# Layer 1's GLU, u and short-conv projections: three 256-column matmuls a block become one of 512 columns and one of 256

## Chip, cores and metric

The kernel runs on one core of one Trainium2 chip. The metric is the device time of one execution in microseconds; the time before is the median of three runs. On the core five engines work side by side: TensorE (PE, whose weight loads are listed apart as PEld), VectorE (DVE), ScalarE (ACT), GpSimd (POOL) and SyncE (SP), which issues the DMAs. TensorE multiplies a stationary block of at most 128 x 128 with moving columns and writes into PSUM, of which one bank holds 512 fp32 columns of 128 partitions. VectorE and ScalarE read PSUM and write SBUF.

## What is computed

A two-layer encoder trunk on 256 positions with 2048 features, in fp32. The part that matters here is the first half of each layer: one input projection `h @ w_in`, whose 4288 columns are split among four mixers.

```python
IN_WIDTHS = (2 * W_G, Q_LORA, KV_LORA, MLA_ROPE, W_G, W_G, W_G, 2 * W_G)   # W_G = 512
h = layer_norm(x) * (1.0 + scale_m) + shift_m
proj = h @ w_in[l]
uv, q_c, kv_c, k_r, sb, sc, sh, ag = jnp.split(proj, IN_SPLITS, axis=-1)
y_a = gmlp_mixer(uv, ...)               # gelu(u) * (W_s LN(gelu(v)) + b)
y_b = mla_mixer(q_c, kv_c, k_r, ...)    # latent attention, 4 heads
y_c = short_conv_mixer(sb, sc, sh, w)   # sb * conv3(sc * sh)
y_d = conformer_conv(ag, ...)           # silu(LN(conv31(a * sigmoid(g))))
y = jnp.concatenate([y_a, y_b, y_c, y_d], axis=-1) @ w_out[l]
x = layer_norm(ALPHA * x + (1.0 + gate_m) * y, post_mix_g[l], post_mix_b[l])
```

Then a gated FFN follows (`ffn_w_up`, a width-3 conv on the gate, SiLU, `ffn_w_down`), with a post-norm of the same kind. The modulation vectors (shift, scale, gate) come from `silu(c) @ w_mod[l]`.

## The kernel before

**Products in three terms.** fp32 products run on TensorE in a faster 32-bit format (`F32R`). For this each weight tile and each activation tile is split into a high part (a cast to F32R on ScalarE, line 460 for weights, 479 for activations) and a low part (the rest, a subtraction on VectorE, lines 461 and 480). A product is high x high + high x low + low x high. Weights arrive as a 1 MB raw tile of 128 partitions x 2048 columns (`weights`, DMA on line 446, four buffers shared with the modulation's weights), and are split into two tiles of 1024 columns; there are four buffers for the high and four for the low ones.

**Activations.** `act_pair` holds two K tiles of the transposed, normalised input `hT` in one tile, ordered (K tile, high or low, 256 positions). So the high and low part of one K tile lie side by side in 512 columns.

**Groups.** Layer 1's `mixers` runs the input projection as groups over 16 K tiles (2048 features), each followed by a function that takes its PSUM tiles:

- V (`first_group`): 512 columns of the gMLP's v, in plain fp32, laid into the norm that ends layer 0
- D: the 1024 columns `ag` (`mix_d`: sigmoid of g, times a, then 31 conv taps for each of four channel blocks, put on the background list)
- U: 512 columns of u (`mix_u`: GELU; `mix_v`: the spatial gating)
- B: 704 columns of the latents (`latent_group`; `mix_b`: the whole attention)
- C: the 1024 columns `sc` and `sh` (`mix_c`: their product, then the width-3 conv)
- E: 512 columns `sb` (`mix_e`: times C's result)

D, U, C and E use `group` (line 482). Its channel blocks of 128 columns take 256 PSUM columns each, two blocks to a bank, and for each K tile and block it issues the three terms as three matmuls of 256 columns (lines 506 to 508). D and C hold four banks and read units of two K tiles x 1024 columns; U and E hold two and read units of four K tiles x 512. The FFN's up projection uses `group2` (line 533) instead: 512 weight columns in units of four K tiles, one bank for each of the four blocks. Per K tile and block it issues a matmul of the high weights with both halves of the activations (512 columns: high x high on the left, high x low on the right) and one of the low weights with the high activations (256 columns, added on the left). Afterwards ScalarE copies the right half out (`second`, line 1339) and VectorE adds it to the left (lines 1346 and 1376). In a unit, blocks 0 and 1 go through all four K tiles before blocks 2 and 3.

**Order.** `stream` issues a unit's load and splits, then the products of the unit before, then a share of modulation work (`pump`, by `RATES`: in layer 1 one step a unit in D, none in U, B and C, 0.9 in E) and up to `bg` items of the background list (`STEPS`). A group's finishing function is issued after the first load of the next group. The engines' instruction streams are ordered at compile time by a list scheduler that follows this order as priority and moves on to other ready work where an instruction would wait in its model; each engine then runs its own stream strictly in order. A modulation step (line 240) multiplies a 128 x 2048 tile of `w_mod` into a sum on VectorE.

**Buffers.** The pool `accp` has six PSUM banks for groups and output products, `msp` two for small things. The pool `slot` has eleven SBUF tiles of 128 x 1024, `tmp` four of 128 x 512. After E, `out_proj` (line 666) starts with four accumulator banks, two for each half of the positions, and multiplies the four mixers' results in the order a, b, c, d.

Layer 0 goes through `by_pieces` and keeps its own form.

Of the kernel before, what the change touches and what calls it, by code (L numbers as in the profile page):

```python
# [9 lines left out]
AF = mybir.ActivationFunctionType  # L10
ALU = mybir.AluOpType
# [3 lines left out]
D = 2048  # L15
S = 256
# [9 lines left out]
C_UV, C_Q, C_SB, C_SC, C_AG = 0, 1024, 1728, 2240, 3264  # L26
# [24 lines left out]
def encoder_kernel(ctx: ExitStack, tc: tile.TileContext, A: dict, consts: bass.AP, out: bass.AP):  # L51
# [17 lines left out]
    def tmp_tile(name):  # L69
        return tmpp.tile([P, 512], F32, tag="tmp", name=name)  # L70
# [13 lines left out]
    def slot(name, dtype=F32):  # L84
        return slotp.tile([P, 1024], dtype, tag="slot", name=name)
# [396 lines left out]
    def group(w, c0, width, name, then, ntm=0, nk=2, hF=None, bg=0, spare=0):  # L482

        ncm = (width - 512 * ntm) // P
        box = {}

        def products(item, u):
            if u == 0:  # L490
                box["c"] = [acc_tile(f"{name}_c{i}") for i in range((ncm + 1) // 2)]
                box["t"] = [[acc_tile(f"{name}_t{t}{i}") for i in range(ntm)] for t in range(2)]
                box["h"] = list(hT)
            for part in (range(0, min(4, ncm)), range(4, ncm)):
                for k, (hi, lo) in enumerate(item):
                    kt = u * nk + k
                    st, sp = kt == 0, kt == KT - 1
                    for i in part:
                        o = box["c"][i // 2][:, (i % 2) * S : (i % 2 + 1) * S]
                        off = slice(i * P, (i + 1) * P)  # L500
                        first = st and i % 2 == 0
                        if lo is None:
                            mm(o, hi[:, off], hF(kt), first, sp)
                        else:
                            xh, xl = (h[:, kt % 2, :] for h in box["h"][kt // 2][:2])
                            mm(o, hi[:, off], xh, first, False)
                            mm(o, hi[:, off], xl, False, False)
                            mm(o, lo[:, off], xh, False, sp)
            for k, (hi, lo) in enumerate(item):
                kt = u * nk + k  # L510
                st, sp = kt == 0, kt == KT - 1
                for i in range(ntm):
                    off = slice(ncm * P + i * 512, ncm * P + (i + 1) * 512)
                    for t in range(2):
                        tok = slice(t * P, (t + 1) * P)
                        o = box["t"][t][i]
                        if lo is None:
                            mm(o, hF(kt)[:, tok], hi[:, off], st, sp)
                        else:
                            xh, xl = (h[:, kt % 2, tok] for h in box["h"][kt // 2][:2])  # L520
                            mm(o, xh, hi[:, off], st, False)
                            mm(o, xh, lo[:, off], False, False)
                            mm(o, xl, hi[:, off], False, sp)

        def load(u, spare=spare):
            return weights(w, u * nk, nk, c0, width, hF is not None, spare if u == 0 else 0)

        def end():
            then(box["c"], box["t"])

        return KT // nk, load, products, end, bg

    def group2(w, c0, name, then, bg=0, spare=0):


        nk = 4
        box = {}

        def products(item, u):
            if u == 0:  # L540
                box["c"] = [acc_tile(f"{name}_c{i}") for i in range(4)]
                box["h"] = list(hT)
            for part in (range(0, 2), range(2, 4)):
                for k, (hi, lo) in enumerate(item):
                    kt = u * nk + k
                    both = box["h"][kt // 2][2][:, kt % 2, :, :]
                    for i in part:
                        o = box["c"][i]
                        off = slice(i * P, (i + 1) * P)
                        mm(o, hi[:, off], both.rearrange("p h t -> p (h t)"), kt == 0, False)  # L550
                        mm(o[:, :S], lo[:, off], both[:, 0, :], False, kt == KT - 1)

        def load(u):
            return weights(w, u * nk, nk, c0, 512, False, spare if u == 0 else 0)

        return KT // nk, load, products, lambda: then(box["c"]), bg
# [60 lines left out]
    def run(g):  # L617
        units, load, products, end, bg = g
        for u in range(units):
            stream(lambda: load(u), lambda item, u=u: products(item, u), bg)  # L620
        pending.append(end)
# [223 lines left out]
    def mixers(l, w_in, Y, hF=None, between=None):  # L845
# [10 lines left out]
        def mix_d(cps, _):  # L856
            glu = slot("gluD").rearrange("p (j s) -> p j s", j=4)
            for b in range(2):
                sg = tmp_tile("sg")
                act.activation(out=sg, in_=cps[2 + b], func=AF.Sigmoid)  # L860
                dve.tensor_tensor(
                    out=glu[:, 2 * b : 2 * b + 2, :],
                    in0=cps[b].rearrange("p (j s) -> p j s", j=2),
                    in1=sg.rearrange("p (j s) -> p j s", j=2),
                    op=ALU.mult,
                )
            yd = slot("convD").rearrange("p (j s) -> p j s", j=4)
            def tap(j, k):
                if k == 30:
                    ident_act(yd[:, j, :], glu[:, j, :], CW(30, j), CB(j))  # L870
                else:
                    dve.scalar_tensor_tensor(  # L872
                        out=yd[:, j, 30 - k :],
                        in0=glu[:, j, : S - 30 + k],
                        scalar=CW(k, j),
                        in1=yd[:, j, 30 - k :],
                        op0=ALU.mult,
                        op1=ALU.add,
                    )

            for j in range(4):
                for k in range(30, -1, -1):
                    background.append(lambda j=j, k=k: tap(j, k))
            background.append(lambda: norm_d(yd))
# [38 lines left out]
        def mix_u(cps, _):  # L923
            Y["a"] = slot("ya").rearrange("p (j s) -> p j s", j=4)
            for b in range(2):
                act.activation(
                    out=Y["a"][:, 2 * b : 2 * b + 2, :],
                    in_=cps[b].rearrange("p (j s) -> p j s", j=2),
                    func=AF.Gelu_apprx_tanh,
                )  # L930

        def gelu_v(t, ps):
            if t == 0:
# [229 lines left out]
        def mix_c(cps, _):  # L1163
            ch = slot("chC").rearrange("p (j s) -> p j s", j=4)
            for b in range(2):
                sc = tmp_tile("sc")
                act.copy(sc, cps[b])
                dve.tensor_tensor(
                    out=ch[:, 2 * b : 2 * b + 2, :],
                    in0=cps[2 + b].rearrange("p (j s) -> p j s", j=2),  # L1170
                    in1=sc.rearrange("p (j s) -> p j s", j=2),
                    op=ALU.mult,
                )
            yc = Y["c"] = slot("yc").rearrange("p (j s) -> p j s", j=4)
            for j in range(4):
                act.activation(out=yc[:, j, :], in_=ch[:, j, :], func=AF.Copy, scale=SW(2, j))
                for k in range(2):
                    dve.scalar_tensor_tensor(
                        out=yc[:, j, 2 - k :],
                        in0=ch[:, j, : S - 2 + k],  # L1180
                        scalar=SW(k, j),
                        in1=yc[:, j, 2 - k :],
                        op0=ALU.mult,
                        op1=ALU.add,
                    )

        def mix_e(cps, _):
            yc = Y["c"]
            for b in range(2):
# [4 lines left out]
                    op=ALU.mult,  # L1194
                )

        if hF is not None:
            return by_pieces(l, w_in, hF, between, mix_d, mix_u, gelu_v, mix_v, mix_b, mix_c, mix_e)
        phase(l, "V")
        first_group(w_in, C_UV + 512, gelu_v)  # L1200
        phase(l, "D")
        run(group(w_in, C_AG, 1024, f"D{l}", mix_d))

        def mix_uv(cps, _):
            mix_u(cps, None)
            mix_v()

        phase(l, "U")
        run(group(w_in, C_UV, 512, f"U{l}", mix_uv, nk=4, bg=STEPS[l]["U"]))
        phase(l, "B")  # L1210
        run(latent_group(w_in, C_Q, f"B{l}", mix_b, bg=STEPS[l]["B"]))
        phase(l, "C")
        run(group(w_in, C_SC, 1024, f"C{l}", mix_c, bg=STEPS[l]["C"]))
        phase(l, "E")
        run(group(w_in, C_SB, 512, f"E{l}", mix_e, nk=4, bg=STEPS[l]["E"]))
        drain_background()

    def by_pieces(l, w_in, hF, between, mix_d, mix_u, gelu_v, mix_v, mix_b, mix_c, mix_e):
# [360 lines left out]
```

## Time and profile before

| | |
|---|---|
| time, median of 3 runs | 2282.23 us (2279.70, 2282.23, 2286.89) |
| profiled execution, span | 2283.6 us (its device time is not given apart) |
| layer 0's FFN up projection | about 480 to 960 us |
| norm between the layers, V | 1190.0 to 1231.7 us |
| layer 1: D, U | 1231.7 to 1278.0, 1278.0 to 1301.5 us |
| layer 1: B, C with the attention | 1301.5 to 1334.8, 1334.8 to 1413.5 us |
| layer 1: E | 1413.5 to 1441.3 us |
| matmuls of the listed groups D, U, C, E in layer 1 | 384 + 192 + 384 + 192 |
| HBM read | 600.11 MB, 264 GB/s over the span |

How to read it: times in the trace are microseconds from the start of the span, durations of single instructions mostly nanoseconds. A group's line gives its source line, engine, operation, tile written and tiles read, shapes and count, then busy time and mean duration, then the idle time before its instructions and what ended it. All matmuls of the products are issued by one helper on line 79, so they are told apart by the tile they write: `D_c`, `U_c`, `B_w` and `B_n`, `C_c`, `E_c` for the groups, `g_c` and `v_c` for the FFN's gate and value, `o` and `d` for the two output projections. A row of the stage table gives for each engine its busy time and number of instructions, then TensorE's granted clock, the DMA engines' busy share and GB/s. Matmuls are pipelined, and their ends are modelled.

### The profile page before, as it was taken

The numbers are of one execution on the slowest core, as the hardware profiler recorded it, in microseconds if no ns is written. First come the engines' busy times: TensorE is split into PE (matmuls) and PEld (weight loads), VectorE is DVE, ScalarE is ACT, GpSimd is POOL, SyncE is SP. The second block draws the span as 40 slices with busy tenths as digits, with TensorE's granted clock in tenths as the row PEclk, the third lists the DMA queues.
The fourth block names the chain that finished last, engine by engine and source line by source line (L and its number), as shares of the span: only waits on it lengthen the run. The fifth ranks groups of instructions, "written<-read, shape, count | busy, mean of one in ns | idle before, by whom it ended". The sixth has DMA issues, their size and how long they took to land. (4 is left out here: it accounts for less than half of the span.)

```text
span 2283.6 us, 29677 instructions
## 1 busy us (share of the span) xinstructions
PE 2218.9 (97%) x11502; PEld 1846.1 (81%) x11502; DVE 1785.1 (78%) x2258; ACT 1056.0 (46%) x1551; POOL 38.8 (2%) x61
## 2 busy tenths in 40 slices
PE   5799999999999999999999999999999999999998
PEld 4687786478888888887886989877888888888886
DVE  6868899588889898998977896887776565665676
ACT  2231241354554554544556444556555554454553
POOL 1000000000000000000000000000000000000000
PEclk9999999999999999999999999999999999999999
DMA  9999879878898989988875664866765556555554
GB/s 348 357 325 329 321 284 378 316 261 322 307 334 302 330 307 329 322 316 297 322 271 191 236 193 161 322 244 227 247 222 184 191 182 200 186 195 190 193 194 148
DMA packets 224565, 604.15 MB, mean 265 GB/s; under 512 B 14548, under 2 KB 27076, under 8 KB 202660
## 3 DMA queue, kind: packets, MB, share of 16 engines
q1 hardware_dynamic: 223576, 601.25, 74.2%
q8 instruction: 90, 1.47, 0.3%
q0 software_dynamic: 848, 1.01, 0.1%
q14 instruction: 51, 0.42, 0.1%
HBM read 600.11 MB, written 2.10 MB: 264 GB/s over the span
## 5 line engine op out<-in xcount | busy, mean ns | idle before, releaser
L461 DVE TENSOR_TENSOR wlo<-wraw,whi 128x1024 fp32r<-128x1024 f32 (+1 forms) x624 | 748.1, 1212 | 307.6 <-ACT whi L460 301.1
L460 ACT CAST whi<-wraw 128x1024 fp32r<-128x1024 f32 (+1 forms) x624 | 649.3, 1046 | 724.5 <-PE g_c L79 198.8
L79 PE MATMUL v_c<-hT,whi 128*128 128x512 f32 x1408 | 491.3, 393 | 0.0
L79 PE MATMUL g_c<-hT,whi 128*128 128x512 f32 x1280 | 446.8, 393 | 0.0
L79 PE MATMUL v_c<-hT,wlo 128*128 128x256 f32 x1408 | 393.9, 280 | 0.0
L79 PE MATMUL d<-whi,a 128*128 128x512 f32 x1344 | 387.7, 390 | 0.0
L240 DVE SCALAR_TENSOR_TENSOR macc<-wmod,cact,macc 128x2048 f32<-128x2048 f32 x150 | 351.7, 2344 | 19.1 <-DMA wmod<-in_w_mod_dram 18.6
L79 PE MATMUL g_c<-hT,wlo 128*128 128x256 f32 x1280 | 358.2, 280 | 0.0
L79 PEld LDWEIGHTS v_c<-hT,whi 128*128 128x128 f32 x1408 | 263.7, 187 | 59.7
L79 PEld LDWEIGHTS d<-whi,a 128*128 128x128 f32 x1344 | 252.8, 188 | 52.5
L79 PEld LDWEIGHTS g_c<-hT,whi 128*128 128x128 f32 x1280 | 239.7, 187 | 54.4
L79 PEld LDWEIGHTS v_c<-hT,wlo 128*128 128x128 f32 x1408 | 265.8, 189 | 0.2
L79 PEld LDWEIGHTS g_c<-hT,wlo 128*128 128x128 f32 x1280 | 241.7, 189 | 0.2
L79 PE MATMUL d<-wlo,a 128*128 128x512 f32 x672 | 233.8, 390 | 1.9 <-DVE wlo L461 1.9
L79 PEld LDWEIGHTS d<-wlo,a 128*128 128x128 f32 x672 | 126.6, 188 | 29.0 <-DVE wlo L461 2.7
L79 PE MATMUL o<-whi,a 128*128 128x512 f32 x352 | 101.7, 396 | 1.4 <-ACT whi L460 1.4
L872 DVE SCALAR_TENSOR_TENSOR convD<-gluD,pm,convD 128x255 f32<-128x255 f32 (+22 forms) x240 | 98.3, 460 | 0.4
L479 ACT CAST a<-g 128x512 fp32r<-128x512 f32 x132 | 81.1, 616 | 35.4 <-PE d L79 32.7
L79 PE MATMUL D_c<-hT,whi 128*128 128x256 f32 x448 | 88.0, 297 | 3.8 <-ACT hT L479 3.0
L480 DVE TENSOR_TENSOR a<-g,a 128x512 fp32r<-128x512 f32 x132 | 87.6, 683 | 1.8 <-ACT a L479 1.8
L604 PE MATMUL first<-wexact,hN 128*128 128x512 f32 x192 | 85.7, 596 | 1.5 <-ACT hN L82 1.2
L240 DVE SCALAR_TENSOR_TENSOR qacc<-wmod,cact,qacc 128x1024 f32<-128x1024 f32 (+1 forms) x75 | 80.2, 1070 | 2.4 <-DMA wmod<-in_w_mod_dram 0.4
(324 smaller groups left out, 2462.5 us busy)
## 6 DMA issues: line engine op xcount, KB each, us to landing
wraw<-in_ffn_w_up_dram SPq DMA_DIRECT2D x168, 1024.0 KB, 5.1
wmod<-in_w_mod_dram SPq DMA_DIRECT2D x160, 1024.0 KB, 6.6
wraw<-in_ffn_w_down_dram SPq DMA_DIRECT2D x88, 1024.0 KB, 5.2
wmod<-in_w_mod_dram SPq DMA_DIRECT2D x64, 512.0 KB, 8.2
wraw<-in_w_in_dram SPq DMA_DIRECT2D x30, 1024.0 KB, 7.1
wexact<-in_w_in_dram SPq DMA_DIRECT2D x52, 512.0 KB, 7.0
wraw<-in_w_out_dram SPq DMA_DIRECT2D x24, 1024.0 KB, 6.8
wexact<-in_w_out_dram SPq DMA_DIRECT2D x16, 512.0 KB, 11.8
```

What stands on the lines that cost most here:

```text
L79: pe.matmul(o, lhsT, rhs, start=start, stop=stop, skip_group_check=True)
L240: i = dve.scalar_tensor_tensor(out=acc, in0=w, scalar=col, in1=acc, op0=ALU.mult, op1=ALU.add)
L460: held(act.copy(hi[:, :m], r), "cast")
L461: i = dve.tensor_tensor(out=lo[:, :m], in0=r, in1=hi[:, :m].bitcast(F32), op=ALU.subtract)
L479: act.copy(hi, src)
L480: dve.tensor_tensor(out=lo, in0=src, in1=hi.bitcast(F32), op=ALU.subtract)
L604: i = pe.matmul(ps, hN[kt // 4][:, kt % 4, t * P : (t + 1) * P], parts[kt], start=kt == 0, stop=kt == KT - 1, skip_group_check=True,)
L872: dve.scalar_tensor_tensor(out=yd[:, j, 30 - k :], in0=glu[:, j, : S - 30 + k], scalar=CW(k, j), in1=yd[:, j, 30 - k :], op0=ALU.mult, op1 ...
```

## The change

In layer 1 alone, D, U, C and E go through `group2`. D is run as two groups of 512 columns, first g (`Dg`), then a (`Da`); C as sc (`Cc`), then sh (`Ch`). The new `joined` copies the right half of each bank into a `tmp` tile and adds the left half, and yields two blocks at a time; the finishing functions use it. `Dg` ends with the sigmoid into the GLU's slot, `Da` multiplies into it and starts the conv; `Cc` ends with its sum in the slot `chC`, `Ch` multiplies into it and starts the short conv. The tails `conv_d` and `conv_c` are the old code under a name. The rates and the number of units stay.

```diff
+            conv_d(glu)
+
+        def joined(cps):
+
+            for b in range(2):
+                t = tmp_tile("second").rearrange("p (j s) -> p j s", j=2)
+                for i in range(2):
+                    act.copy(t[:, i, :], cps[2 * b + i][:, S:])
+                    dve.tensor_tensor(out=t[:, i, :], in0=cps[2 * b + i][:, :S], in1=t[:, i, :], op=ALU.add)
+                yield b, t
+
+        def gated_d(cps):
+            Y["glu"] = slot("gluD").rearrange("p (j s) -> p j s", j=4)
+            for b, t in joined(cps):
+                act.activation(out=Y["glu"][:, 2 * b : 2 * b + 2, :], in_=t, func=AF.Sigmoid)
+
+        def valued_d(cps):
+            glu = Y.pop("glu")
+            for b, t in joined(cps):
+                g = glu[:, 2 * b : 2 * b + 2, :]
+                dve.tensor_tensor(out=g, in0=g, in1=t, op=ALU.mult)
+            conv_d(glu)
+
+        def conv_d(glu):
...
+        def joined_u(cps):
+            Y["a"] = slot("ya").rearrange("p (j s) -> p j s", j=4)
+            for b, t in joined(cps):
+                act.activation(out=Y["a"][:, 2 * b : 2 * b + 2, :], in_=t, func=AF.Gelu_apprx_tanh)
...
+            conv_c(ch)
+
+        def first_c(cps):
+            Y["ch"] = slot("chC").rearrange("p (j s) -> p j s", j=4)
+            for i in range(4):
+                ch = Y["ch"][:, i, :]
+                act.copy(ch, cps[i][:, S:])
+                dve.tensor_tensor(out=ch, in0=cps[i][:, :S], in1=ch, op=ALU.add)
+
+        def second_c(cps):
+            ch = Y.pop("ch")
+            for b, t in joined(cps):
+                c = ch[:, 2 * b : 2 * b + 2, :]
+                dve.tensor_tensor(out=c, in0=c, in1=t, op=ALU.mult)
+            conv_c(ch)
+
+        def conv_c(ch):
...
+        def joined_e(cps):
+            for b, t in joined(cps):
+                c = Y["c"][:, 2 * b : 2 * b + 2, :]
+                dve.tensor_tensor(out=c, in0=c, in1=t, op=ALU.mult)
...
         phase(l, "D")
-        run(group(w_in, C_AG, 1024, f"D{l}", mix_d))
-
-        def mix_uv(cps, _):
-            mix_u(cps, None)
+        run(group2(w_in, C_AG + 512, f"Dg{l}", gated_d))
+        run(group2(w_in, C_AG, f"Da{l}", valued_d))
+
+        def mix_uv(cps):
+            joined_u(cps)
             mix_v()
 
         phase(l, "U")
-        run(group(w_in, C_UV, 512, f"U{l}", mix_uv, nk=4, bg=STEPS[l]["U"]))
+        run(group2(w_in, C_UV, f"U{l}", mix_uv, bg=STEPS[l]["U"]))
         phase(l, "B")
         run(latent_group(w_in, C_Q, f"B{l}", mix_b, bg=STEPS[l]["B"]))
         phase(l, "C")
-        run(group(w_in, C_SC, 1024, f"C{l}", mix_c, bg=STEPS[l]["C"]))
+        run(group2(w_in, C_SC, f"Cc{l}", first_c, bg=STEPS[l]["C"]))
+        run(group2(w_in, C_SC + 512, f"Ch{l}", second_c, bg=STEPS[l]["C"]))
         phase(l, "E")
-        run(group(w_in, C_SB, 512, f"E{l}", mix_e, nk=4, bg=STEPS[l]["E"]))
+        run(group2(w_in, C_SB, f"E{l}", joined_e, bg=STEPS[l]["E"]))
         drain_background()
```

## The prediction

> **What bounds the kernel now.** I read the engine line of the page first, then the busy time of each engine by stage, then the waits of TensorE inside layer 1's mixers, then the timelines at the seams between its groups.
>
> ```profile
> PE 2218.9 (97%) x11502; PEld 1846.1 (81%) x11502; DVE 1785.1 (78%) x2258; ACT 1056.0 (46%) x1551; POOL 38.8 (2%) x61
> ...
> core 0: us, PE busy (x) PEld busy (x) DVE busy (x) ACT busy (x) POOL busy (x), PEclk, DMA share, GB/s
> 480.00:960.00 480.00, 480.00 (x2746) 419.07 (x2745) 429.34 (x474) 250.75 (x362) 0.00 (x0) 1.00 0.89 320
> ...
> 1231.70:1278.00 46.30, 46.30 (x385) 46.06 (x384) 36.61 (x30) 16.38 (x17) 2.11 (x3) 1.00 0.99 368
> 1278.00:1301.50 23.50, 23.50 (x198) 23.50 (x197) 22.68 (x40) 13.52 (x18) 0.00 (x0) 1.00 0.53 157
> 1301.50:1334.80 33.30, 33.08 (x212) 32.82 (x211) 33.20 (x68) 14.61 (x22) 0.00 (x0) 1.00 0.63 186
> 1334.80:1413.50 78.70, 75.77 (x525) 70.02 (x524) 55.22 (x107) 34.32 (x64) 3.52 (x3) 0.98 0.50 167
> 1413.50:1441.30 27.80, 27.53 (x222) 26.97 (x221) 25.26 (x34) 14.30 (x19) 1.61 (x1) 1.00 0.72 260
> 1441.30:1530.00 88.70, 88.70 (x392) 73.20 (x392) 74.10 (x90) 43.60 (x60) 1.31 (x2) 1.00 0.79 289
> ```
>
> The last six stretches are, in order, layer 1's D group (GLU and long conv), U, B (latents), C with the attention laid between its matmuls, E, and the output projection. From 1231.7 to 1441.3 TensorE is idle for 0.2 + 2.9 + 0.3 = 3.4 us of 209.6, at full granted clock. So the stage ends when TensorE has streamed its columns. But VectorE is full in U (22.68 of 23.50) and B (33.20 of 33.30) and nearly full in E, and the DMA share is 0.99 in D: so two other limits lie close behind.
>
> ```profile
> PE ps_kv L1030 <- ACT qg L1036: 2.6, 1, 2.6
> ...
> PE ps_rD L79 <- DVE dgD L912: 0.3, 1, 0.3
> PE ps_mix L79 <- DVE wT L955: 0.2, 1, 0.2
> ```
>
> These waits are the idle time: one in the attention, two small ones. None is at a group's own matmuls.
>
> **The matmuls.** A matmul's listed duration (280 to 393 ns) overlaps its neighbours', so I take the pace from starts.
>
> ```profile
> L79 PE MATMUL U_c<-hT,wlo x64: 283/283/285, 1278.4 to 1301.1; 128*128 128x256 f32 x64
> ...
> L79 PE MATMUL C_c<-hT,whi x134: 278/283/283, 1389.5 to 1413.4; 128*128 128x256 f32 x134
> ...
> 1609.32 22.19 PE v_c L79 x128
> ```
>
> Today each weight block (128 rows of K by 128 columns) costs three matmuls of 256 columns. In U 64 blocks' last matmuls start over 22.7 us: 22.7 / 63 = 360.3 ns a block, 120.1 a matmul. The undisturbed end of C agrees: 134 high-weight matmuls, two a block, in 23.9 us, 23.9 / 133 x 2 = 359.4. The changed form already runs in the FFN: one matmul of 512 columns and one of 256 a block, and the chain of waits has 64 blocks in 22.19 us, 346.7 ns. D, U, C and E hold 16 x (8 + 4 + 8 + 4) = 384 blocks. The saving is 384 x (360.3 - 346.7) = **5.2 us**: 1.7 in D, 0.9 in U, 1.7 in C, 0.9 in E. The dropped instructions' durations (384 x 0.28 = 108 us of listed time) are no saving, since they overlap.
>
> The Trainium skill, in TensorE: Matmul & The Clock Gate, section Back-to-back issue gap, speaks against the change: it gives 262 cycles for 256 columns and 518 for 512, a fixed part of only 6 cycles, so that at 2.4 GHz an estimate by that page is 2.5 x 384 = 1.0 us saved. The trace disagrees: its 512-column matmul takes 346.7 - 120.1 = 226.6 ns, and two short ones 240.2. The measurement decides.
>
> **The added vector work.** The two halves of each bank must now be added: for every group four ScalarE copies and four VectorE adds of 128x256. The FFN has both.
>
> ```profile
> L1339 ACT COPY second<-v_c 128x256 f32<-128x256 f32 x88 | 31.9, 373 | 32.6 <-PE v_c L79 30.5
> ...
> L1376 DVE TENSOR_TENSOR second<-v_c,second 128x256 f32<-128x256 f32 x88 | 34.4, 418 | 9.3 <-ACT second L1339 9.1
> ...
> L240 DVE SCALAR_TENSOR_TENSOR macc<-wmod,cact,macc 128x2048 f32<-128x2048 f32 x150 | 351.7, 2344 | 19.1 <-DMA wmod<-in_w_mod_dram 18.6
> ...
> 1370.08 0.44 DVE L872 SCALAR_TENSOR_TENSOR convD<-gluD,pm,convD 128x226 f32<-128x226 f32 x1
> ...
> 1432.89 1.40 DVE L892 SCALAR_TENSOR_TENSOR convD<-ps_mean,convD 128x256 f32<-128x256 f32 x4
> ```
>
> D and C become two such groups each, so there are six: 24 adds x 0.418 = 10.0 us of VectorE and 24 copies x 0.373 = 9.0 us of ScalarE, less the two 0.59 us copies that C drops. The products, sigmoids and GELUs stay, in number and size. ScalarE is at most 58% busy in these stages, so it hides its share. VectorE's goes: Dg's four adds into D's 9.7 us idle; Da's and U's (3.3 us) into full stages, where they push back the conv taps, which end at 1370.1 and are first needed at 1432.9; C's into 23.5 idle us; and Ch's and E's (3.3 us) into E and the projection's first microseconds. E is the tight one: 25.26 + 1.7 us against a stage that shrinks to 26.9. What stands there too is splits for the projection, which has 14.6 us of VectorE idle, so I take **+0.5**, bounds 0 and +2. In U and B a split could be pushed instead of a tap: taken 0, bounds 0 and +3.3.
>
> **The accumulators.** There are six PSUM banks for groups. Every changed group now holds four; U and E held two. At a seam the next group has two banks free and needs two from the group just ended. Its first two banks carry half a unit, 8 x 346.7 ns = 2.8 us of matmuls. A bank is free after one copy and one add, 0.37 + 0.42 = 0.8 us, or 0.8 + 2.3 = 3.1 with a modulation step ahead in VectorE's queue, which would leave 0.3 uncovered.
>
> ```profile
> L79 PE MATMUL v_c<-hT,whi 128*128 128x512 f32 x1408 | 491.3, 393 | 0.0
> L79 PE MATMUL g_c<-hT,whi 128*128 128x512 f32 x1280 | 446.8, 393 | 0.0
> ```
>
> The FFN has this seam 40 times, and its matmuls never sat idle, modulation steps included (the stretch 480 to 960 above: 480.00 busy of 480.00). So Dg to Da, Da to U, Cc to Ch, Ch to E and E to the projection cost 0 (B hands its four banks to C as before); the upper bound for each is the whole hand-over, four copies and four adds in a row behind a step, 3.2 + 2.3 - 2.8 = 2.7 us. Casts and splits of the next unit queue behind the copies and adds; they run a unit ahead.
>
> U to B is another seam, seen nowhere before, because U left B four banks.
>
> ```profile
> 1301.18 0.60 PE L952 MATMUL ps_wT<-cst,gmlp 128*128 128x128 f32 x4
> 1301.54 0.42 PE L79 MATMUL B_w<-whi,hT 128*128 128x384 f32 x1
> 1301.80 0.30 PE L79 MATMUL B_n<-whi,hT 128*128 128x320 f32 x1
> ```
>
> B touches its second tile with its second matmul, and within a K step all four. With U's four banks in their hands it waits for two. Lower bound 0 (transposes and wide matmuls go ahead), upper 0.37 + 4 x 0.42 = 2.1 us; I take **+0.8**, one copy and one add.
>
> **Loads and waits elsewhere.** Each unit is still 1 MB by one issue, and the number of units, and so of modulation steps and background calls, is unchanged; rows become 2 KB instead of 4 in D and C. The FFN's loads are of that shape and reach 320 GB/s at a share of 0.89, 360 at full share, beside 368 / 0.99 = 372 in D. D needs two 1 MB tiles a unit, 2.097 / 0.368 = 5.70 us, against 46.3 / 8 = 5.79 now and 16 x 0.3467 = 5.55 after: the transfers could hold back 8 x 0.15 = 1.2 us.
>
> ```profile
> 1260.96 2.36 DVE L461 TENSOR_TENSOR wlo<-wraw,whi 128x1024 fp32r<-128x1024 f32 x2 [1.21 <-ACT whi L460]
> ...
> 1225.18 2.49 DVE L480 TENSOR_TENSOR hT<-hN,hT 128x512 fp32r<-128x512 f32 x4
> 1231.67 0.80 PE L79 MATMUL D_c<-hT,whi 128*128 128x256 f32 x2
> ```
>
> The seventh unit's splits end at 1263.3 and its products start at 1231.7 + 6 x 5.79 = 1266.4: three microseconds of lead cover it, so 0, upper bound 1.2. Dg walks through all of the normalised input in 22 us instead of 46, but its last splits end at 1227.7, before the first product: 0. In the attention the filler between its steps gets 4% shorter: 0, between -2.9 (the wait goes) and +1.
>
> **Sum.** -5.2 + 0.5 + 0.8 = **-3.9 us**. The profiled span is 2283.6; no other time is given for that execution, and the runs' median is 2282.2, 1.4 below it. The span would be 2279.7, the median **2278.3**.
>
> **Rivals.**
> - VectorE becomes the bound of U, B and E. For: its shares there. Against: taps can move. All ten added microseconds exposed: -5.2 + 10.0 = +4.8, 2287.0.
> - Slower: TensorE waits for banks at the six seams, because copies and adds stand behind steps and splits in ScalarE's and VectorE's fixed order. For: D runs a modulation step in every unit, E nearly, and E's seams carry the norm of D besides. Against: the FFN's 40 seams. Price 5 x 2.7 + 2.1 - 5.2 = +10.4, 2292.6; it outweighs the saving from 0.9 us a seam, and shows as slower from 2.0.
> - Faster: every bound falls well and the attention's 2.9 us wait closes: -5.2 - 2.9 = -8.1, 2274.1. For: the order there is made anew. Against: that wait is on a chain through ScalarE and GpSimd that the change doesn't touch.
> - The change saves nothing, since a short matmul costs half a long one: +1.3, 2283.5. The two paces speak against it; the page cited above is for it.
>
> **How the numbers follow.** Forecast 0.50, VectorE bound 0.16, banks 0.15, faster 0.15, no saving 0.04. The median can be told from no change by about 0.3%, 6.8 us, which is also the spread of the three runs. Faster by that (below 2275.4): 0.12 of the faster rival and 0.06 of the forecast, 0.18. Slower (above 2289.1): 0.13 of the banks and 0.03 of VectorE, 0.16. Between: 0.66. The forecast's own range is 2274 to 2283. The bounds give 2274.1 at one end and 2292.6 at the other; with the medians' spread at the low side and the last tail of the banks cut off, 2272 to 2290.
>
> **What would show it.** Right: C's undisturbed blocks at 347 ns, TensorE's idle time from D's start to the projection's first matmul below 5 us, and that stretch at 206 us instead of 209.6. A wait of B_n on the add of U's bank near 0.8 us. Wrong: waits of Da, U, Ch, E or `o` on the joining adds (the banks), waits on low-weight splits in U, B or E (VectorE), or on casts in D with the loads late (transfers). The forecast falls if the stretch is longer than before, or if a block keeps 360 ns.

## The result, and the profile after

The changed kernel takes 2281.49 us (median of 22 runs, 2271.21 to 2284.04), the kernel before 2285.51 (22 runs beside them, 2279.70 to 2291.34). The ratio is 0.9978, with a 95% interval of 0.9969 to 0.9986: by that ratio 5.0 us faster, 3.2 to 7.1 (the medians themselves differ by 4.0). The interval does not reach 1, so this is a gain, though one below the 0.3% that the prediction set as the least that can be told.

The engine line of the page of the changed kernel (span 2271.7 us) shows the 384 dropped matmuls, 24 more VectorE and 22 more ScalarE instructions:

```profile
PE 2206.6 (97%) x11118; PEld 1817.5 (80%) x11118; DVE 1792.9 (79%) x2282; ACT 1060.8 (47%) x1573; POOL 38.9 (2%) x61
```

The same table by stage as in the prediction, now cut at the first product of D, U, B, C, E and the projection:

```profile
1225.30:1270.10 44.80, 44.80 (x259) 39.11 (x258) 38.05 (x35) 20.10 (x26) 2.44 (x3) 1.00 0.98 353
1270.10:1292.60 22.50, 22.50 (x134) 19.88 (x133) 22.41 (x41) 11.62 (x17) 0.00 (x0) 1.00 0.69 217
1292.60:1326.90 34.30, 33.03 (x211) 32.74 (x210) 34.20 (x71) 16.23 (x26) 0.00 (x0) 1.00 0.61 181
1326.90:1402.40 75.50, 73.11 (x399) 61.40 (x398) 59.46 (x118) 35.03 (x69) 3.23 (x3) 1.00 0.53 174
1402.40:1429.30 26.90, 26.57 (x157) 23.21 (x156) 24.20 (x33) 13.12 (x21) 1.60 (x1) 1.00 0.72 254
1429.30:1518.00 88.70, 88.70 (x393) 73.20 (x392) 76.72 (x96) 46.08 (x64) 1.27 (x2) 1.00 0.81 293
```

From D's start to the projection it is 204.0 us instead of 209.6: D -1.6, U -0.9, **B +1.0**, **C -3.3**, E -0.8 (the same cut of before gives 46.4, 23.4, 33.3, 78.8 and 27.7). D, U and E gave what the pace promised, in this profile. B, whose matmuls the change leaves alone, grew; C gave twice its share. The projection is as long as before, 88.7 us. The other 6.3 us between the two profiled spans lie ahead of D, where both kernels do the same; they belong to the two executions (in the second and third profiles of the changed kernel, shown further down, D starts 3.4 and 4.3 us later).

The waits of TensorE in this stretch of the changed kernel (total, times, longest, in us) show why B grew:

```profile
PE ps_kv L1059 <- ACT qg L1065: 2.2, 1, 2.2
PE B_w L79 <- DVE wlo L461: 1.3, 1, 1.3
PE ps_rD L79 <- DVE dgD L936: 0.3, 1, 0.3
```

No group waits for a joining add. The attention's wait stayed. New is one wait of B for a low-weight split. And the pace, by the starts of the matmuls of U and of C's second half:

```profile
L79 PE MATMUL U_c<-hT,whi x64: 391/391/392, 1270.1 to 1291.9; 128*128 128x512 f32 x64
...
L79 PE MATMUL Ch_c<-hT,whi x64: 390/391/392, 1380.2 to 1402.0; 128*128 128x512 f32 x64
```

Both need 21.8 us for 63 steps, 346 ns a block. This is not so in every execution. In the second and third profiles of the same kernel U needs 22.3 us (here the second):

```profile
L79 PE MATMUL U_c<-hT,whi x64: 395/398/403, 1274.3 to 1296.6; 128*128 128x512 f32 x64
```

That is 354 ns a block, and only half of the saving. The wide form has two paces; the last section returns to this.

### The profile page after: what moved, and what is told of

Same layout as the page of the kernel before. It is cut to its first block, busy times and chain, and to the rows that moved or that the text cites. A ratio compares the mean times of both kernels' runs of the same rounds, so it can differ in the third digit from the quotient of the medians.

```text
span 2271.7 us, 28947 instructions
## 1 busy us (share of the span) xinstructions
PE 2206.6 (97%) x11118; PEld 1817.5 (80%) x11118; DVE 1792.9 (79%) x2282; ACT 1060.8 (47%) x1573; POOL 38.9 (2%) x61
## 5 line engine op out<-in xcount | busy, mean ns | idle before, releaser
L896 DVE SCALAR_TENSOR_TENSOR convD<-gluD,pm,convD 128x255 f32<-128x255 f32 (+27 forms) x240 | 98.7, 456 | 0.4
L79 PEld LDWEIGHTS o<-whi,a 128*128 128x128 f32 x352 | 66.6, 190 | 17.1 <-ACT whi L460 2.9
```

The lines of the kernel that those rows point to most:

```text
L79: pe.matmul(o, lhsT, rhs, start=start, stop=stop, skip_group_check=True)
L896: dve.scalar_tensor_tensor(out=yd[:, j, 30 - k :], in0=glu[:, j, : S - 30 + k], scalar=CW(k, j), in1=yd[:, j, 30 - k :], op0=ALU.mult, op1 ...
```

## The experiments

Edits are against the changed kernel. Each execution also has a mean granted TensorE clock, between 0.987 and 0.993, and the time follows it: a line common to all 177 executions for which it is listed, with one offset for each kernel, falls by 1.48 +- 0.30 us for each 0.001 of clock. The last column is that offset against before, so it compares the kernels at equal clock (95% intervals; the two sets of runs of one kernel are taken together). A kernel that waits less could itself get a higher clock, and the line would hide that part; the last experiment bears on this. Each ratio is to runs of before beside the kernel in question. The experiments ran on three chips, on which before's medians were 2285.24, 2285.37 and 2285.60.

| kernel | median us (runs) | ratio to before | mean clock | at equal clock, us |
|---|---|---|---|---|
| before | 2285.40 (73) | | 0.9896 | 0 |
| changed | 2281.49 (22) | 0.9978 (0.9969 to 0.9986) | 0.9903 | -3.4 +- 1.1 |
| changed, third set | 2282.36 (11) | 0.9983 (0.9973 to 0.9993) | 0.9900 | with the line above |
| short matmuls everywhere | 2313.17 (4) | 1.0128 (1.0108 to 1.0148) | 0.9908 | +29.0 +- 2.6 |
| short matmuls in layer 1's groups | 2285.59 (12) | 1.0002 (0.9990 to 1.0014) | 0.9902 | +0.4 +- 1.6 |
| joins twice | 2284.91 (10) | 1.0000 (0.9986 to 1.0013) | 0.9894 | -1.1 +- 1.7 |
| no halves | 2283.80 (10) | 0.9997 (0.9984 to 1.0011) | 0.9888 | -2.7 +- 1.7 |
| fewer taps in U | 2279.58 (12) | 0.9975 (0.9965 to 0.9986) | 0.9899 | -5.5 +- 1.2 |
| fewer taps in U, again | 2281.41 (11) | 0.9977 (0.9966 to 0.9989) | 0.9895 | with the line above |
| fewer taps in U and B | 2280.12 (12) | 0.9981 (0.9971 to 0.9992) | 0.9897 | -4.9 +- 1.6 |

**The pace: the wide matmul split into two short ones**, in every use of `group2` (the FFN too), and then in layer 1's six groups alone. The work is the same, in three matmuls a block, and everything else of the change stays.

```diff
-                        mm(o, hi[:, off], both.rearrange("p h t -> p (h t)"), kt == 0, False)
+                        mm(o[:, :S], hi[:, off], both[:, 0, :], kt == 0, False)
+                        mm(o[:, S:], hi[:, off], both[:, 1, :], False, kt == KT - 1)
```

> Changes how the 512-column matmul is issued, in every group2, the FFN's included: two matmuls of 256 columns into the two halves of the same bank. Joins, banks and loads stay. 3072 blocks (384 in layer 1's input projection, 2688 in the FFN). Pace theory (13.6 ns saved per block by joining two short matmuls): 3072 x 13.6 = 41.8 us slower than the changed kernel, some 1.016 of the kernel before, and 64 blocks of v_c in 23.05 us instead of 22.19. Rival (a fixed part of 2.5 ns per matmul, as the Trainium skill's page has it): +7.7 us, about equal to 1.001 of the kernel before, 64 blocks in 22.35 us.

The second kernel has these lines only under `if name[0] in "DUCE":`.

> The same split of the wide matmul, only in layer 1's six groups, so that the joins, the hand-over of banks and the halves of C and D remain but the pace is that of before. Pace theory: +5.2 us on the changed kernel, the stretch from the first product of D to the first of the output projection 209 us instead of 204.0, and the ratio to the kernel before near 1.000. Rival (the gain comes from the new grouping and order, not from the pace): the stretch stays within 1 us of 204.

The chain of waits (start, length, tile, matmuls) has the third FFN group of layer 1, 64 blocks, first in the changed kernel, then with the split:

```profile
1597.36 22.19 PE v_c L79 x128
```

```profile
1620.10 23.04 PE v_c L79 x192
```

That is 346.7 and 360.0 ns a block, the paces that the prediction gave the two forms, in the same group and with the same loads. With the split in layer 1 alone the stretch from D to the projection is back at 210.9 us (D 46.5, U 23.4, C 78.4), and at equal clock the time is that of before, +0.4 +- 1.6. So the matmul's form carries the whole gain. Here TensorE waits for a split in E (1.9 us, E 29.7) and not in B: where the joins bite depends on the order, and it is why the stretch is longer than the 209 us expected. The total of the first kernel, 32 us above the changed one, is less than 3072 x 13.3 ns = 41 us. Layer 1's 21 FFN groups show their full 21 x 0.85 = 17.9. Layer 0's show less: from their first product to the first of the down projection they take 488.9 us (477.4 to 966.3), against 472.5, 474.6 and 474.6 in the three profiles of the changed kernel, 14.3 to 16.4 more, because there some groups of the wide form run at its slower pace. The stretch from there to D is 274.2 us, against 276.4 to 278.1; why was not followed.

The rule of the Trainium skill that the prediction weighed (TensorE: Matmul & The Clock Gate, section Back-to-back issue gap: 262 and 518 cycles, given there for a matmul by itself) would make the first kernel 3072 x 2.5 ns = 7.7 us slower, an estimate by that page. The measurement decides: 256 columns take 120.0 ns and 512 take 346.7 - 120.0 = 226.7, so a matmul with its weight load has a fixed part of 2 x 120.0 - 226.7, about 13 ns. The FFN's down projection, all of 512 columns, confirms the long one: 239.69 us for 1056 matmuls in a row, 227.0 ns each.

**The vector work: every join done again**, a second copy and add for each of the 24, into a scratch tile that nothing reads.

```diff
                     dve.tensor_tensor(out=t[:, i, :], in0=cps[2 * b + i][:, :S], in1=t[:, i, :], op=ALU.add)
+                    again = tmp_tile("again")[:, :S]
+                    act.copy(again, t[:, i, :])
+                    dve.tensor_tensor(out=again, in0=t[:, i, :], in1=again, op=ALU.add)
```

> Every joining copy and add of layer 1's six groups is done a second time into a scratch tile: 24 more copies on ScalarE and 24 more adds on VectorE, 10 us of VectorE. If VectorE's free time hides the joins: the stretch D to the output projection grows by 0 to 2 us (204 to 206), most of it in B, where TensorE already waits 1.3 us for a split. If VectorE is the bound of U, B and E: it grows by 5 to 10 us. If bank hand-overs were exposed: waits of TensorE at the seams on the adds.

The waits of TensorE and the row of B in this kernel:

```profile
PE B_w L79 <- DVE wlo L461: 3.2, 1, 3.2
...
PE Da_c L79 <- DVE wlo L461: 0.3, 1, 0.3
```

```profile
1302.40:1341.50 39.10, 35.90 (x211) 35.34 (x210) 36.49 (x77) 17.33 (x28) 0.00 (x0) 0.91 0.53 161
```

The joins cost time at one place, B, by a wait of 1.3 us; doubled, it is 3.2. That is 1.9 more, and the time at equal clock is up by 2.3 (from -3.4 to -1.1, two intervals that overlap). B is longer by more than that, since the clock fell behind the wait (0.91 in the row). The whole stretch is 211.7 us, 7.7 more than the changed kernel's and outside the 204 to 206 expected; but the clock takes 0.09 x 39.1 in B and, at 0.98, 0.02 x 77.7 in C, 5.1 together, and 2.6 are left. Some ten more microseconds of VectorE cost two to three: most of the joins lie where VectorE has room.

**The seams: the groups without halves**, all four blocks through the four K tiles together, so that all banks are done only near the group's end (U's first copy starts 0.7 us before its last product, instead of 2.8).

```diff
-            for part in (range(0, 2), range(2, 4)):
+            for part in (range(0, 4),) if name[0] in "DUCE" else (range(0, 2), range(2, 4)):
```

> In layer 1's six groups each K tile goes through all four blocks, instead of blocks 0 and 1 going through a unit's four K tiles first. All four banks then end with the group, and all four are wanted at once by the next. If the halves are what hides the hand-over of banks: TensorE waits about 1 to 2 us at each of six seams, 6 to 10 us in all on the stretch. If the scheduler's reordering hides it in any case: at most 1 us, no wait at a seam over 0.5 us.

```profile
PE ps_kv L1059 <- ACT qg L1065: 2.2, 1, 2.2
PE B_w L79 <- DVE wlo L461: 1.3, 1, 1.3
PE ps_mix L79 <- DVE wT L984: 0.4, 1, 0.4
PE ps_rD L79 <- DVE dgD L936: 0.3, 1, 0.3
```

Still no wait of a group for a bank. The stretch is 205.1 us against 204.0, and at equal clock the two kernels can't be told apart. The halves are not what makes the seams free. How the seam from U to B goes in the changed kernel, by its timeline (start, length, engine):

```profile
1289.32 0.72 ACT L874 COPY second<-U_c 128x256 f32<-128x256 f32 x2 [1.76 <-PE U_c L79]
...
1289.84 0.41 DVE L875 TENSOR_TENSOR second<-U_c,second 128x256 f32<-128x256 f32 x1
...
1290.55 0.41 DVE L875 TENSOR_TENSOR second<-U_c,second 128x256 f32<-128x256 f32 x1
...
1292.13 0.28 PE L79 MATMUL U_c<-hT,wlo 128*128 128x256 f32 x1
1292.24 0.60 PE L981 MATMUL ps_wT<-cst,gmlp 128*128 128x128 f32 x4
1292.60 0.42 PE L79 MATMUL B_w<-whi,hT 128*128 128x384 f32 x1
1292.86 0.30 PE L79 MATMUL B_n<-whi,hT 128*128 128x320 f32 x1
```

The adds of U's first two blocks end at 1290.96, 1.2 us before U's last product starts. With the two free banks B then has its four. Without the halves the first two adds start at 1295.18 and 1295.89, and B's four tiles, in the order of the code, are first written at 1295.29, 1295.55, 1296.34 and 1296.52: it is closer, but the two free banks and adds that follow their copies at once are still enough for TensorE not to wait.

**The wait in B: fewer conv taps in U.** VectorE's timeline in B of the changed kernel ahead of that wait:

```profile
1296.54 0.89 DVE L461 TENSOR_TENSOR wlo<-wraw,whi 128x704 fp32r<-128x704 f32 x1
1297.34 0.46 DVE L896 SCALAR_TENSOR_TENSOR convD<-gluD,pm,convD 128x233 f32<-128x233 f32 x1
1297.83 0.42 DVE L1005 TENSOR_TENSOR mixed<-ps_mix,gmlp 128x256 f32<-128x256 f32 x1
...
1301.61 0.68 DVE L1011 TENSOR_TENSOR ya<-ya,mixed 128x512 f32<-128x512 f32 x1
1302.21 1.21 DVE L896 SCALAR_TENSOR_TENSOR convD<-gluD,pm,convD 128x227 f32<-128x227 f32 x3
1303.33 1.69 DVE L461 TENSOR_TENSOR wlo<-wraw,whi 128x704 fp32r<-128x704 f32 x2
```

Between 1297.4 and 1303.3 no split is made: U's gating steps and taps stand there, and B's product, ready at 1303.0, waits until 1304.27. The edit takes two background items a unit from U and gives C one more.

```diff
-    dict(U=7, B=4, C=4, E=8, up=2),
+    dict(U=5, B=4, C=5, E=8, up=2),
```

> The changed kernel with fewer conv taps issued in U (5 a unit instead of 7) and more in C (5 instead of 4). If the 1.3 us wait of B for a low-weight split is VectorE's backlog of taps and joins: the wait goes or falls below 0.5 us, B takes 33.0 to 33.5 us instead of 34.3, the stretch D to the output projection some 203 us. If the wait comes from somewhere else (the gating's own VectorE work in B): it stays at 1 us or more.

```profile
PE ps_kv L1059 <- ACT qg L1065: 2.4, 1, 2.4
PE ps_rD L79 <- DVE dgD L936: 0.3, 1, 0.3
PE E_c L79 <- DVE wlo L461: 0.2, 1, 0.2
```

```profile
1300.10:1332.90 32.80, 32.80 (x211) 32.80 (x210) 32.64 (x66) 16.24 (x26) 0.00 (x0) 1.00 0.66 189
```

The wait is gone, and B takes 32.8 us instead of 34.3, TensorE busy in all of it. The stretch in this one profile is 204.3 us, not the 203 expected: D, U, C and E are each 0.3 to 0.6 longer than in the first profile of the changed kernel, and U runs at the slower pace (22.2 us for 63 steps). A second try takes taps from B as well (`U=4, B=3, C=7, E=8`):

> The same, further: 4 taps a unit in U, 3 in B, 7 in C. Backlog theory: no wait in U or B, B at 33.0, VectorE no longer full there; C's VectorE, 59 of 75 us busy, takes 24 more taps (10 us), and if they stand ahead of the attention's steps, C grows by up to 2 us. Rival as before: the wait in B stays.

B is 32.9 us there, without a wait; nothing more is won. The first version was run again:

> U with five background items a unit instead of seven, again, beside the changed kernel on the same chip. Theory (the joining work costs time only through B's wait for a low-weight split, 1.3 us, which fewer taps ahead of it take away): no wait of B on a split, B at 32.8 us, and at equal clock 1 to 2 us faster than the changed kernel, -4.5 to -5.5 against before. Rival (the wait in B is hidden by a later one, the attention's): the same time as the changed kernel, -3.6 against before, with C longer by what B is shorter.

Again no wait in B, and 32.8 us. Both sets together are 2.0 +- 1.4 us faster than the changed kernel at equal clock, so the wait was not hidden by the attention's. By plain ratios the step is not settled: 0.9975 and 0.9977 against 0.9978 and 0.9983. At equal clock it is the fastest version, though the one with fewer taps in B as well can't be told from it.

**The clock: further profiles of both kernels.** Before and the changed kernel, as they are:

> The kernel before, a second profile. In the first its TensorE clock fell to 0.67 and 0.76 for 6 us after the 2.6 us wait in the attention, which cost C about 1.6 us. If the fall belongs to the kernel: again a mean clock of 0.98 in C and a stretch of 209.6. If it is chance: in some profiles the clock stays at 1.00 and C takes 77.2.

> The changed kernel, a second profile. If its steady clock in C (wait of 2.2 us, no fall) belongs to the kernel: again 1.00 and C at 75.5. If it is chance: C at up to 77, with a clock of 0.98. The wait of 1.3 us in B should come again, since the order is fixed.

> The changed kernel again, to tell how much of its gain hangs on the granted clock. So far all runs together lie on a line of -1.5 us per 0.001 of mean granted clock; at equal clock the change is worth -3.6 +- 1.3 us against before, while the plain means differ by 4.6. Theory (the change is worth its matmul pace less a wait in B, and the rest of C's gain is the clock of the profiled execution): at equal clock again -3 to -4.5 us; the profile has the low-weight wait of 1.2 to 1.3 us in B; C lasts 75.5 us when its clock is 1.00 and about 77 when it is 0.98. Rival (the change itself lifts the clock in C, because it shortens or moves the attention's wait): the mean clock of its runs is above that of the runs of before by 0.0007 or more again, and C's clock is 1.00.

The second profile of before has a stretch of 212.5 us with C at 81.8 (clock 0.94) and a span of 2283.5; the second at the changed kernel 206.9 with C at 76.9 (0.98) and 2278.1; the third 208.4, with C at 79.1:

```profile
1297.60:1331.80 34.20, 33.05 (x212) 32.76 (x209) 34.10 (x71) 16.30 (x26) 0.00 (x0) 1.00 0.61 181
1331.80:1410.90 79.10, 76.69 (x398) 63.37 (x397) 59.09 (x118) 34.99 (x69) 3.24 (x3) 0.96 0.50 167
```

B has its 34.2 or 34.3 us, and its wait, in all three profiles of the changed kernel. C goes from 75.5 to 79.1 with the clock from 1.00 to 0.96, so the change doesn't hold the clock up, and the mean clock of these 11 runs, 0.9900, is 0.0004 above that of all of before's runs and 0.0002 above that of the runs beside them (0.9898). That speaks for chance; a small lift isn't excluded.

## Why the prediction was right, and where it was not

**The pace term** (-5.2) is shown as the cause: both paces were measured, the stage lengths of D, U and E fell by 1.6, 0.9 and 0.8, and undoing the form of the matmul alone undid the gain. Its size is an upper bound, since the prediction knew one pace of the wide form and there are two. In the second and third profiles D, U and E together are 1.7 and 2.4 us shorter than before, not 3.3. The slower pace stood in the trace of before too: one group of layer 0's FFN has 22.3 us for its 63 steps (931.0 to 953.3).

**C** gave 3.3 us where 1.7 was forecast. The prediction called the stretch of before one at full granted clock, though its own row has 0.98 in C: 0.02 x 78.8 us is a loss of 1.6. The first profile of the changed kernel had none. At full clock C gains 78.8 - 1.6 - 75.5 = 1.7. The rest is the clock of two executions.

**VectorE's term** (+0.5 in E, and the pushed split in U or B taken as 0) was the step that failed in place and size. In the changed kernel E lost nothing; only with short matmuls did it wait. The cost was the pushed split in B, 1.2 us on average over three profiles (1.3, 1.2, 1.1), inside the bounds of 0 to 3.3 that the prediction kept for it. B's row before, VectorE at 33.20 of 33.30 us, had said so; "taps can move" was true only of an order with fewer taps in U. The rival with all ten microseconds exposed is out: doubling the joins cost two to three.

**The seams** (+0.8) cost 0. The sum took U's four banks to be all in the hands of the copies and adds when B starts. But U's first two blocks end half a unit before its last, and their banks were free again before U's end: the same cover as at the other seams. With the two that U never held, they are B's four. The rival of the six seams is out.

**The sum** came out near -3.9 by errors that cancel, which was luck: -5.2 + 1.2 + 0 = -4.0. The stretch without the clock's loss in C is 5.6 - 1.6 = 4.0 us shorter in the first profile of the changed kernel. In the second and third, with 0.02 x 76.9 and 0.04 x 79.1 taken off in the same way, it is 2.6 and 2.8 shorter, for the most part by the slower pace. The runs at equal clock, 3.4 +- 1.1, lie between. The plain medians differ by 4.0, and the ratio, which isn't that of the medians, gives 5.0; about 1 of that is clock, since its mean was 0.0007 higher, if that was chance.

**The predicted time**, 2278.3, is 3.2 below 2281.5, and this is the base. The prediction set the span of 2283.6 beside a median of three runs, 1.4 lower. Later executions whose time and span are both listed took about 2 us more than their spans (2273.86 for 2271.7), and over 22 runs before is at 2285.51, 3.3 above the median of three. (Those three runs spread over 7.2 us, a little more than the 6.8 that the prediction gave them.)

**The faster rival** is out as it was put: the attention's wait went from 2.6 to 2.2 us and stayed in every kernel. Of D's loads (bounds 0 to 1.2) little was seen: D ran with a DMA share of 0.98, without a wait, at 44.8 us. In the other two profiles it took 45.6 and 45.0, the first of them with a wait of 0.2 for a low-weight split at a share of 0.99; whether a late load stood behind it was not followed.

## What to carry to other kernels

Where one stationary block meets two moving tiles that lie side by side, one wide matmul saves the fixed part of the second, here 13 ns or, at the slower pace, about half of it, and the price is paid on the engine that joins the halves. Price that work at the stage where the engine is already full, even if it is issued in another: the question is which instruction that TensorE waits for stands behind it in the queue. Then move optional work (here conv taps) out of the stretch ahead of that instruction.

## What was not expected of the hardware

The granted clock falls after a gap of TensorE of little more than 2 us, in some executions and not in others, and this moves a single profile by as much as the whole change. TensorE's rows in slices of 3 us around the attention's wait, first in the first profile of the changed kernel, then in the third:

```profile
1330.00:1333.00 3.00, 1.79 (x11) 1.30 (x9) 1.75 (x5) 0.56 (x2) 2.93 (x2) 1.00 0.22 84
1333.00:1336.00 3.00, 2.03 (x13) 1.48 (x13) 1.55 (x5) 3.00 (x6) 0.30 (x1) 1.00 0.00 0
1336.00:1339.00 3.00, 3.00 (x14) 2.40 (x14) 3.00 (x5) 0.90 (x3) 0.00 (x0) 1.00 0.00 0
```

```profile
1335.00:1338.00 3.00, 1.65 (x11) 1.15 (x9) 1.62 (x5) 0.56 (x3) 2.89 (x3) 1.00 0.21 79
1338.00:1341.00 3.00, 2.15 (x12) 1.69 (x12) 1.67 (x5) 3.00 (x6) 0.22 (x1) 0.86 0.00 0
1341.00:1344.00 3.00, 3.00 (x7) 1.75 (x7) 3.00 (x5) 0.60 (x3) 0.00 (x0) 0.50 0.00 0
1344.00:1347.00 3.00, 3.00 (x9) 2.37 (x8) 3.00 (x9) 0.18 (x1) 0.00 (x0) 0.50 0.88 276
```

Each time TensorE is idle for 2.2 us (1.21 + 0.97 and 1.35 + 0.85). Once the clock stays at 1.00; once it is at 0.86, 0.50 and 0.50, a loss of 3 x (0.14 + 0.50 + 0.50) = 3.4 us, nearly all of the 3.6 by which C's 79.1 stand above 75.5. The Trainium skill (TensorE: Matmul & The Clock Gate, section What's actually happening) says that the clock halves after an idle window of about 3.4 us, and that the windows run freely. The half clock and the dependence on chance agree with these rows; a gap of 2.2 us does not fill such a window, so the length does not.

The other surprise is the second pace. A block of one 512-column and one 256-column matmul takes either 347 or 353 to 354 ns, for whole groups at a time and at a granted clock of 1.00: U takes 21.8 us for its 63 steps in the first profile of the changed kernel and 22.3 in the second and third. Three matmuls of 256 columns show one pace: 22.7 us for U's 63 steps in both profiles of before and in the kernel with short matmuls everywhere. What sets the pace isn't shown; so the saving of a block is 13 ns or about half of that, and a prediction should hold both.
